# A diffusion backbone with an expert mixer: who makes the low parts of the weight tiles

## The chip, the cores and the metric

The kernel runs on one core of one Trainium2 chip. The metric is the device time of one execution in microseconds. The core has five engines with a queue of instructions each: TensorE (PE in the profile, its weight loads PEld), VectorE (DVE), ScalarE (ACT), GpSimd (POOL) and SyncE (SP). Each works through its own queue in order and waits at semaphores for the others.

## The reference

The model is a stack of two layers over a latent stream of 512 tokens and a context stream of 256 tokens, each token 1024 numbers in float32. A layer normalises and modulates, mixes tokens (a gated linear recurrence beside a short convolution, between an input and an output projection), and then runs an expert mixer, the PEER part:

```python
def peer_ffn(h, wq, subkeys, u, v):
    qr = (h @ wq).reshape(bsz, t, PEER_HEADS, 2, PEER_HALF)
    scores = jnp.einsum('bthpd,hpkd->bthpk', qr, subkeys)
    s1, i1 = lax.top_k(scores[..., 0, :], PEER_TOPK)
    s2, i2 = lax.top_k(scores[..., 1, :], PEER_TOPK)
    ...
    top, pos = lax.top_k(cand, PEER_TOPK)       # 16 of 16 x 16 sums
    eidx = jnp.take_along_axis(cidx, pos, axis=-1)
    gate = jax.nn.softmax(top, axis=-1)
    ...
        act = jax.nn.gelu(jnp.einsum('ted,td->te', u[ek], hk), approximate=False)
        return jnp.einsum('te,ted->td', gk * act, v[ek])
```

Each token chooses 8 x 16 = 128 of 16384 experts; an expert is one row of `u` and one row of `v`. The context stream is needed in layer 0 in full, and in layer 1 only for the final states of the recurrence.

## The kernel before

**Precision by splitting.** TensorE multiplies in a rounded format (`float32r`). So every operand is split into a high part (the rounded copy) and a low part (the rest), and each product is three matmuls: high by high, high by low, low by high. For a weight tile this is done by `weights` (L289 to L298): SP's queue loads 512 KB into `wraw` (L293), ScalarE rounds it into `whi` (L295), and a subtraction on one engine makes `wlo` (L297). Each of the three has three buffers. `weights` is called for 624 tiles of 128 x 1024: by `proj` for the projections of mixing and of the expert queries, by `experts_in` for the rows of `u`, by `dense` for the rows of `v`.

**Two ways through the experts.** For most token blocks of 128 (three or four of a layer) the mixer is computed densely, over all experts: `gates` makes a table of gate values by token and expert (one-hot tiles `oA`, `oB`, L759 to L776, multiplied on TensorE into `gps` and written to memory as `gd`); `experts_in` multiplies the tokens by two tiles of `u` and applies the GELU (`A`); `dense` multiplies `A` by the gates (L809), splits it into `Wh` and `Wl` (L812, L813), and for each group of 8 expert tiles and each of 8 output slices multiplies by a tile of `v` (L820 to L822) and adds the sum to the residual `resx` (L824). Some of the `experts_in` work is done ahead, during `gates`, and kept in memory (`ad`).

For the remaining blocks (two context blocks in layer 0, one latent block in layer 1) `gather_block` fetches the chosen rows: for each of 128 choices GpSimd issues an indirect transfer of one row of `u` for every token (L856, into three buffers `gr` and one `gs`), and VectorE multiplies it with the tokens and sums (L863); then the same for `v`, with an accumulating VectorE operation (L872). These 256 gathers for a block run beside `gates` and `dense` of the same layer. The result is added to the residual at L877 and L879.

**Who sets the order.** The program is written stage by stage, but a planner places the instructions in each engine's queue by a modelled timeline and priorities; weight tiles have a raised priority (`WPRIO`), and gathers fill in. What an engine is asked to do therefore changes the order planned for all of them. The order of the streams in the mixing of layer 1 puts the latent stream first.

**What the change touches.** Two constants, `POOL_LO` and `POOL_UT`, decide in `dense` and in `experts_in` which engine makes a tile's low part; without them it is VectorE.

Of the kernel before, what the change touches and what calls it, by code (L numbers as in the profile page):

```python
# [9 lines left out]
F = mybir.dt.float32  # L10
# [5 lines left out]
OP = mybir.AluOpType  # L16
# [25 lines left out]
U0 = 96  # L42
EARLY = (1, 0)
LASTK = [4, 5, 6, 7, 0, 1, 2, 3]
POOL_LO = True
POOL_UT = True


class Streams:
# [7 lines left out]
class Kern:  # L57
# [9 lines left out]
            kw["reuse_waits"] = "tile"  # L67
        return (stack or self.ctx).enter_context(self.tc.tile_pool(name=name, bufs=bufs, **kw))

    # ---------------------------------------------------------------- constants  # L70
    def setup(self):
        nc, a = self.nc, self.a
        self.tables()
# [99 lines left out]
        tag = self.banks[self.turn % len(self.banks)]  # L173
        return self.psum(shape, tag, 2 if tag == "ga" else 1, name)

    # ---------------------------------------------------------------- adaLN
    def mods(self, l, cols, pool, tag, bufs, ptags=("mo",)):
        nc = self.nc
        for ct in cols:
            ptag = ptags[ct % len(ptags)]  # L180
            pp = self.psum([P, 512], ptag, 2 if ptag == "ga" else 1, "pmod")
            pt, pm = pp[:, :256], pp[:, 256:].rearrange("p (a b) -> p a b", b=P)
            for kh in range(0, KC, 4):
                tags = tag.split()
                w = pool.tile([P, 4, 256], F, name="wmod", tag=tags[(2 * ct + kh // 4) % len(tags)], bufs=bufs)
                dma = nc.sync.dma_start(w, self.a["w_mod"][l, ct, :, kh:kh + 4])
                for k in range(4):
                    nc.tensor.matmul(pt[32 * k:32 * k + 32], self.cond[:, kh + k, :], w[:, k],
                                     start=kh == 0, stop=kh > 0, skip_group_check=True)
            part = self.wp.tile([P, 256], F, name="mpart", tag="mpart", bufs=1)  # L190
            nc.scalar.activation(part, pt, AF.Copy)
            for j in range(2):
                nc.tensor.matmul(pm[:, j], part[:, j * P:(j + 1) * P], self.selm, start=True, stop=True)
            c = ct * 2
            m = self.mod[l][:, c:c + 2, :]
            b = self.bmod[:, l, c:c + 2].unsqueeze(2).to_broadcast([P, 2, 2])
            nc.vector.tensor_tensor(m, pm[:, :, 0:2], b, op=OP.add)
            g, h = divmod(ct, 4)
            if g in (1, 4):
                n = 0 if g == 1 else 1  # L200
                s = self.scl[l][:, n, 2 * h:2 * h + 2]
                gb = self.ng[:, 2 * l + n, 2 * h:2 * h + 2].unsqueeze(2).to_broadcast([P, 2, 2])
                nc.vector.tensor_scalar(s, m, 1.0, None, op0=OP.add)
                nc.vector.tensor_tensor(s, s, gb, op=OP.mult)
        return dma.ins

    # ---------------------------------------------------------------- norms
    def rsqrt_rows(self, st, n, scale, name):
        nc = self.nc
        v = self.sm.tile([P, n], F, name=name + "v", tag="rv", bufs=2)  # L210
        s = self.sm.tile([P, n], F, name=name + "s", tag="rs", bufs=2)
        r = self.sm.tile([P, n], F, name=name + "r", tag="rr", bufs=2)
        nc.vector.tensor_scalar(v, st, scale, EPS, op0=OP.mult, op1=OP.add)
        nc.scalar.activation(s, v, AF.Ln)
        nc.scalar.activation(r, s, AF.Exp, scale=-0.5)
        nc.vector.scalar_tensor_tensor(s, v, 0.5, r, op0=OP.mult, op1=OP.mult)
        nc.vector.tensor_tensor(s, s, r, op=OP.mult)
        nc.vector.tensor_scalar(s, s, -1.0, 1.5, op0=OP.mult, op1=OP.add)
        nc.vector.tensor_tensor(r, r, s, op=OP.mult)
        return r  # L220
# [64 lines left out]
                eng = nc.gpsimd if POOL_NM and c % 2 else nc.vector  # L285
                eng.scalar_tensor_tensor(lo[:, c], t, sh[:, c:c + 1], hi[:, c].bitcast(F), op0=OP.add, op1=OP.subtract)

    # ---------------------------------------------------------------- projections
    def weights(self, src, eng=None):  # L289
        nc = self.nc  # L290
        with self.tc.high_priority(offset=WPRIO):
            raw = self.wp.tile([P, KC, P], F, name="wraw", tag="wraw", bufs=3)
            nc.sync.dma_start(raw, src)  # L293
            hi = self.wp.tile([P, KC, P], R, name="whi", tag="whi", bufs=3)
            nc.scalar.activation(hi, raw, AF.Copy)  # L295
            lo = self.wp.tile([P, KC, P], R, name="wlo", tag="wlo", bufs=3)
            (eng or nc.vector).tensor_tensor(lo, raw, hi.bitcast(F), op=OP.subtract)  # L297
        return hi, lo  # L298

    def mm3(self, out, w, a, n=None, order=range(KC)):  # L300
# [22 lines left out]
            out.append((pt[:, TX:TX + TC], slice(0, TC)))  # L323
        return out

    # ---------------------------------------------------------------- mixer
    def mixer(self, l):
        nc, a, tc = self.nc, self.a, self.tc
        last = l == self.depth - 1
# [252 lines left out]
        for src, sl in self.parts(pt, wc):  # L582
            nc.vector.tensor_tensor(self.oc.at(4 + j, sl.start, sl.stop), o[:, sl], src, op=OP.mult)

    # ---------------------------------------------------------------- PEER
    def top16(self, pool, vals, ixs, src, n):
        nc = self.nc
        w = pool.tile([P, n], F, name="mr", tag=f"mr{n}", bufs=1)
        nc.vector.max(vals[:, 0:8], src)
        nc.vector.max_index(ixs[:, 0:8], vals[:, 0:8], src)  # L590
        nc.vector.match_replace(w, vals[:, 0:8], src, NEG)
        nc.vector.max(vals[:, 8:16], w)
        nc.vector.max_index(ixs[:, 8:16], vals[:, 8:16], w)
# [187 lines left out]
    def experts_in(self, l, ap, hx, jp, nt):  # L781
        nc = self.nc
        pt = self.psum([P, 2, 512], "pj", 2, "p1")
        for t in range(2):
            w = self.weights(self.a["ut"][l, 2 * jp + t], self.nc.gpsimd if t and POOL_UT else None)
            self.mm3(pt[:, t, :nt], w, hx, nt)
        A = ap.tile([P, 2, nt], F, name="A", tag="A", bufs=3)
        self.gelus[0] = nc.scalar.activation(A, pt[:, :, :nt], AF.Gelu).ins  # L788
        return A

    def dense(self, l, es, ap, gd, ad, hx, nt):
        nc, a = self.nc, self.a
        dp = self.pool(f"pd{l}", stack=es)
        NG = 8
        for g in range(P // NG):
            ws = []
            for jp in range(NG // 2):
                j = g * NG + 2 * jp
                if j % 4 == 0:
                    gt = dp.tile([P, nt // 32, 4, 32], F, name="gt", tag="gt", bufs=2)  # L800
                    nc.sync.dma_start(gt.rearrange("p c i t -> p (c i t)"), gd[j // 4].rearrange("p c i t -> p (c i t)"))
                if j // 2 in AHEAD_SET[l]:
                    A = ap.tile([P, 2, nt], F, name="A", tag="A", bufs=3)
                    nc.sync.dma_start(A, ad[AHEAD_SET[l].index(j // 2)])
                else:
                    A = self.experts_in(l, ap, hx, j // 2, nt)
                for t in range(2):
                    av = A[:, t].rearrange("p (c t) -> p c t", t=32)
                    nc.vector.tensor_tensor(av, av, gt[:, :, j % 4 + t, :], op=OP.mult)  # L809
                wh = dp.tile([P, 2, nt], R, name="Wh", tag="Wh", bufs=NG // 2)  # L810
                wl = dp.tile([P, 2, nt], R, name="Wl", tag="Wl", bufs=NG // 2)
                nc.scalar.activation(wh, A, AF.Copy)  # L812
                nc.vector.tensor_tensor(wl, A, wh.bitcast(F), op=OP.subtract)  # L813
                ws.append((wh, wl))
            for c in range(KC):
                hi, lo = self.weights(a["vt"][l, c, g], nc.gpsimd if c % 2 and POOL_LO else None)
                pt = self.bank([P, nt], "p2")
                for j in range(NG):
                    wh, wl = (x[:, j % 2] for x in ws[j // 2])
                    nc.tensor.matmul(pt, hi[:, j], wh, start=j == 0, stop=False)  # L820
                    nc.tensor.matmul(pt, hi[:, j], wl, start=False, stop=False)  # L821
                    nc.tensor.matmul(pt, lo[:, j], wh, start=False, stop=j == NG - 1)  # L822
                dst = self.res.x[:, c, :nt]
                nc.vector.scalar_tensor_tensor(dst, pt, self.mod[l][:, 5 * KC + c, 0:1], dst, op0=OP.mult, op1=OP.add)  # L824
# [53 lines left out]
                dst = self.res.at(c, b * P, (b + 1) * P)  # L878
                nc.vector.scalar_tensor_tensor(dst, pt, self.mod[l][:, 5 * KC + c, s:s + 1], dst, op0=OP.mult, op1=OP.add)  # L879

    # ---------------------------------------------------------------- whole
    def final(self):
        nc = self.nc
        with ExitStack() as es:
# [91 lines left out]
```

## Time and profile before

| | |
|---|---|
| median of 3 runs | 4328.59 us |
| runs | 4332.73, 4328.59, 4319.31 us |
| span of the profiled execution | 4317.6 us, mean granted TensorE clock 0.969 |
| busy: TensorE, VectorE, ScalarE, GpSimd | 3993.6, 3522.3, 1747.0, 1854.1 us |
| low parts on VectorE | 368, 514.6 us |
| low parts on GpSimd | 256, 645.1 us |
| indirect transfers issued by GpSimd | 768 |
| moved to and from memory | 984.57 MB, mean 228 GB/s |

The profile gives the profiled execution from its first to its last instruction: its own time is that span, and what lies around it is seen only in the difference of 11.0 us to the median of the runs. An engine's busy time counts an instruction from its start to its end, also while it waits inside for something that it shares with another engine. The views that follow name instructions by line, engine and operation, with the tile written and the tiles read (`wlo<-wraw,whi`), the number of them after an x, and, in the views of groups, the total busy time, the mean in ns, and the idle time of the engine just before them with what ended it.

### The profile page before, as it was taken

The numbers are of one execution on the slowest core, as the hardware profiler recorded it, in microseconds if no ns is written. First come the engines' busy times: TensorE is split into PE (matmuls) and PEld (weight loads), VectorE is DVE, ScalarE is ACT, GpSimd is POOL, SyncE is SP. The second block draws the span as 40 slices with busy tenths as digits, with TensorE's granted clock in tenths as the row PEclk, the third lists the DMA queues.
The fourth block names the chain that finished last, engine by engine and source line by source line (L and its number), as shares of the span: only waits on it lengthen the run. The fifth ranks groups of instructions, "written<-read, shape, count | busy, mean of one in ns | idle before, by whom it ended". The sixth has DMA issues, their size and how long they took to land.

```text
span 4317.6 us, 59354 instructions
## 1 busy us (share of the span) xinstructions
PE 3993.6 (92%) x21357; PEld 3441.2 (80%) x21357; DVE 3522.3 (82%) x6416; ACT 1747.0 (40%) x2919; POOL 1854.1 (43%) x1180
## 2 busy tenths in 40 slices
PE   7999999989997999999989899979899989999997
PEld 5888778777885777777777778857899989999996
DVE  4766659999988999888788868758985788888987
ACT  4444332368772222222222245433598423333332
POOL 0211100244443566777667712110212257667675
PEclk9999999999998999999999999989999999999998
DMA  6444122489898898888888821213466679889896
GB/s 229 140 150 149 62 68 74 156 277 303 292 303 306 307 339 324 298 311 296 303 296 299 297 73 57 66 60 95 146 206 204 210 274 330 319 326 326 322 323 209
DMA packets 382167, 984.57 MB, mean 228 GB/s; under 512 B 30384, under 2 KB 161712, under 8 KB 377520
## 3 DMA queue, kind: packets, MB, share of 16 engines
q1 hardware_dynamic: 271280, 578.06, 39.1%
q0 software_dynamic: 110592, 402.70, 26.6%
q8 instruction: 169, 2.77, 0.3%
q14 instruction: 126, 1.03, 0.1%
HBM read 883.39 MB, written 97.26 MB: 227 GB/s over the span
## 4 chain that ended last, share of the span: by engine, by line
PE 46%; DVE 24%; DMA 11%; issue 9%; POOL 6%; ACT 3%; POOLq 0%; SPq 0%; DVEq 0%; ACTq 0%
PE p L822 5%; PE p L821 5%; PE p L820 5%; PE pj L304 5%; PE pj L305 5%; PE pj L306 5%; DMA gr<-in_v,picki 4%; DMA gr<-in_u,picki 4%; POOL wlo L297 3%; PE p L304 3%; PE p L305 3%; PE p L306 3%; DVE wlo L297 3%; POOL gr L856 2%; PE gps L775 2%
## 5 line engine op out<-in xcount | busy, mean ns | idle before, releaser
L295 ACT ACTIVATE whi<-wraw 128x1024 fp32r<-128x1024 f32 x624 | 654.5, 1057 | 1300.2 <-PE p L821 670.7
L297 POOL TENSOR_TENSOR wlo<-wraw,whi 128x1024 fp32r<-128x1024 f32 x256 | 645.1, 2521 | 913.1 <-ACT whi L295 329.9
L820 PE MATMUL p<-Wh,whi 128*128 128x512 f32 (+1 forms) x2048 | 753.4, 373 | 81.4 <-DVE resx L824 43.3
L822 PE MATMUL p<-Wh,wlo 128*128 128x512 f32 (+1 forms) x2048 | 755.1, 372 | 40.9 <-POOL wlo L297 24.9
L821 PE MATMUL p<-Wl,whi 128*128 128x512 f32 (+1 forms) x2048 | 759.7, 372 | 27.0 <-DVE Wl L813 26.9
L306 PE MATMUL p<-hxh,wlo 128*128 128x512 f32 (+1 forms) x2048 | 757.2, 370 | 15.0 <-POOL wlo L297 8.9
L304 PE MATMUL p<-hxh,whi 128*128 128x512 f32 (+1 forms) x2048 | 755.7, 369 | 0.7 <-ACT A L788 0.7
L305 PE MATMUL p<-hxl,whi 128*128 128x512 f32 (+1 forms) x2048 | 754.9, 369 | 0.0
L297 DVE TENSOR_TENSOR wlo<-wraw,whi 128x1024 fp32r<-128x1024 f32 x368 | 514.6, 1398 | 98.4 <-ACT whi L295 96.7
L856 POOL DMA_INDIRECT gr<-in_u,picki x312 | 412.3, 1322 | 414.3 <-DVE gr L863 321.6
L863 DVE SCALAR_TENSOR_TENSOR gr<-gr,htok 128x1024 f32<-128x1024 f32 x312 | 448.1, 1446 | 93.8 <-DMA gr<-in_u,picki 93.6
L872 DVE SCALAR_TENSOR_TENSOR acc<-gr,gw,acc 128x1024 f32<-128x1024 f32 x285 | 463.7, 1627 | 67.2 <-DMA gr<-in_v,picki 64.3
L856 POOL DMA_INDIRECT gr<-in_v,picki x288 | 400.2, 1390 | 269.4 <-DVE acc L872 190.3
L820 PEld LDWEIGHTS p<-Wh,whi 128*128 128x128 f32 x2048 | 393.1, 193 | 143.7 <-ACT Wh L812 46.3
L822 PEld LDWEIGHTS p<-Wh,wlo 128*128 128x128 f32 x2048 | 395.0, 193 | 100.0 <-POOL wlo L297 35.6
L821 PEld LDWEIGHTS p<-Wl,whi 128*128 128x128 f32 x2048 | 395.3, 193 | 80.0 <-DVE Wl L813 38.5
L306 PEld LDWEIGHTS p<-hxh,wlo 128*128 128x128 f32 x2048 | 388.3, 190 | 60.2 <-POOL wlo L297 13.2
L304 PEld LDWEIGHTS p<-hxh,whi 128*128 128x128 f32 x2048 | 388.6, 190 | 39.4 <-ACT A L788 1.0
L305 PEld LDWEIGHTS p<-hxl,whi 128*128 128x128 f32 x2048 | 388.5, 190 | 38.8
L812 ACT ACTIVATE Wh<-A 128x1024 fp32r<-128x1024 f32 (+1 forms) x128 | 122.0, 955 | 466.8 <-DVE A L809 429.6
L775 PE MATMUL gps<-oA,oB 128*128 128x128 f32 x1792 | 255.9, 279 | 32.3 <-DVE oA L767 23.9
L775 PEld LDWEIGHTS gps<-oA,oB 128*128 128x128 f32 x1792 | 245.1, 192 | 49.7 <-issue 11.5
(316 smaller groups left out, 7024.1 us busy)
## 6 DMA issues: line engine op xcount, KB each, us to landing
wraw<-in_ut SPq DMA_DIRECT2D x256, 512.0 KB
wraw<-in_vt SPq DMA_DIRECT2D x256, 512.0 KB
gd<-stg SPq DMA_DIRECT2D x28, 2048.0 KB
wmod<-in_w_mod SPq DMA_DIRECT2D x96, 512.0 KB
wraw<-in_w_in SPq DMA_DIRECT2D x64, 512.0 KB
gt<-gd SPq DMA_DIRECT2D x32, 1024.0 KB
gt<-gd SPq DMA_DIRECT2D x32, 768.0 KB
ad<-A SPq DMA_DIRECT2D x34, 512.0 KB
```

The source lines that it names most:

```text
L295: nc.scalar.activation(hi, raw, AF.Copy)
L297: (eng or nc.vector).tensor_tensor(lo, raw, hi.bitcast(F), op=OP.subtract)
L304: nc.tensor.matmul(out, wh[:, k], ah[:, k, :n], start=i == 0, stop=False)
L305: nc.tensor.matmul(out, wh[:, k], al[:, k, :n], start=False, stop=False)
L306: nc.tensor.matmul(out, wl[:, k], ah[:, k, :n], start=False, stop=i == KC - 1)
L775: nc.tensor.matmul(pt[:, s], B[:, s4 + s], A[:, s4 + s], start=True, stop=True)
L820: nc.tensor.matmul(pt, hi[:, j], wh, start=j == 0, stop=False)
L821: nc.tensor.matmul(pt, hi[:, j], wl, start=False, stop=False)
L822: nc.tensor.matmul(pt, lo[:, j], wh, start=False, stop=j == NG - 1)
L856: nc.gpsimd.indirect_dma_start(out=t, out_offset=None, in_=src, in_offset=bass.IndirectOffsetOnAxis(ap=eidx[:, e:e + 1], axis=0))
L863: nc.vector.scalar_tensor_tensor(u, u, 1.0, htok, op0=OP.mult, op1=OP.mult, accum_out=act[:, e:e + 1])
L872: nc.vector.scalar_tensor_tensor(acc, v, w[:, e:e + 1], acc, op0=OP.mult, op1=OP.add)
```

## The change

Every low part of a weight tile is made by VectorE. The two constants go, `weights` loses its choice of engine, and GpSimd keeps in these stages only the issues of the indirect transfers (and the small operations of the recurrence that it had). Comments that were changed beside it are left out.

```diff
-POOL_LO = True
-POOL_UT = True
...
-    def weights(self, src, eng=None):
+    def weights(self, src):
...
-            (eng or nc.vector).tensor_tensor(lo, raw, hi.bitcast(F), op=OP.subtract)
+            nc.vector.tensor_tensor(lo, raw, hi.bitcast(F), op=OP.subtract)
...
-            w = self.weights(self.a["ut"][l, 2 * jp + t], self.nc.gpsimd if t and POOL_UT else None)
+            w = self.weights(self.a["ut"][l, 2 * jp + t])
...
-                hi, lo = self.weights(a["vt"][l, c, g], nc.gpsimd if c % 2 and POOL_LO else None)
+                hi, lo = self.weights(a["vt"][l, c, g])
```

Before, the second of each pair of `u` tiles and every odd output slice of `v` went to GpSimd: 128 + 128 of the 624 tiles.

## The prediction

> **What bounds the kernel now.** First the page: span, busy shares, and the chain of work that ended last.
>
> ```profile
> span 4317.6 us, 59354 instructions
> PE 3993.6 (92%) x21357; PEld 3441.2 (80%) x21357; DVE 3522.3 (82%) x6416; ACT 1747.0 (40%) x2919; POOL 1854.1 (43%) x1180
> PE 46%; DVE 24%; DMA 11%; issue 9%; POOL 6%; ACT 3%; POOLq 0%; SPq 0%; DVEq 0%; ACTq 0%
> ```
>
> TensorE leads, VectorE is close behind, and GpSimd, although less than half busy, holds 6% of the chain. Second, the busy time by stretch. I cut the span at the stages: 850 to 1320 makes the gate tables of layer 0, 1320 to 2480 is its dense expert stage, 3100 to 3440 makes the gate tables of layer 1, 3440 to the end is its dense stage. The second fence is the same view for the weight tile `wlo` alone.
>
> ```profile
> core 0: us, PE busy (x) PEld busy (x) DVE busy (x) ACT busy (x) POOL busy (x), PEclk, DMA share, GB/s
> 850.00:1320.00 470.00, 423.12 (x2302) 360.63 (x2300) 432.73 (x787) 332.01 (x745) 212.04 (x145) 0.97 0.89 299
> 1320.00:2480.00 1160.00, 1062.22 (x4455) 851.58 (x4456) 1023.13 (x1181) 293.23 (x287) 767.48 (x482) 0.96 0.86 305
> 3100.00:3440.00 340.00, 329.03 (x2120) 325.57 (x2121) 241.61 (x584) 255.10 (x557) 74.17 (x29) 0.99 0.66 207
> 3440.00:4318.00 878.00, 811.13 (x4451) 778.65 (x4449) 758.48 (x838) 270.57 (x289) 584.22 (x347) 0.97 0.84 301
> ```
>
> ```profile
> 850.00:1320.00 470.00, 170.41 (x422) 80.96 (x422) 33.12 (x28) 65.88 (x27) 0.97 0.89 299
> 1320.00:2480.00 1160.00, 589.21 (x1482) 285.99 (x1482) 131.66 (x93) 231.28 (x93) 0.96 0.86 305
> 3100.00:3440.00 340.00, 159.17 (x459) 87.43 (x459) 35.32 (x29) 74.17 (x29) 0.99 0.66 207
> 3440.00:4318.00 878.00, 494.88 (x1471) 279.28 (x1470) 156.31 (x91) 229.97 (x91) 0.97 0.84 301
> ```
>
> In the first two stretches VectorE is busy for 92% and 88%. In 3100 to 3440 TensorE is (97%), and VectorE has 98 us to spare. GpSimd makes 27, 93, 29 and 91 low parts there: 240 of its 256.
>
> Third, the order of time around 2060 us (rows of the two engines, sorted by start).
>
> ```profile
> 2058.86 2.37 POOL L297 TENSOR_TENSOR wlo<-wraw,whi 128x1024 fp32r<-128x1024 f32 x1
> 2058.87 3.45 DVE L297 TENSOR_TENSOR wlo<-wraw,whi 128x1024 fp32r<-128x1024 f32 x1
> 2063.39 1.22 DVE L863 SCALAR_TENSOR_TENSOR gs<-gs,htok 128x1024 f32<-128x1024 f32 x1
> 2063.73 1.69 POOL L856 DMA_INDIRECT gr<-in_u,picki  x1 [2.51 <-DVE gr L863]
> 2070.04 0.94 POOL L856 DMA_INDIRECT gr<-in_u,picki  x1 [0.31 <-issue]
> ```
>
> A low part of VectorE that starts with one of GpSimd takes 3.45 us, the 2.37 us of the other and then its own 1.1. An indirect issue does no such harm: the operation beside it kept 1.22 us, and it was the issue that took 1.69 instead of 0.94. So what costs VectorE time is GpSimd's subtraction. How much it costs is the mean over the undisturbed median.
>
> ```profile
> L297 DVE TENSOR_TENSOR wlo<-wraw,whi x368: 1169/1217/4662, 42.7 to 4270.5; 128x1024 fp32r<-128x1024 f32 x184
> L297 POOL TENSOR_TENSOR wlo<-wraw,whi x256: 2346/2410/4405, 753.8 to 4272.7; 128x1024 fp32r<-128x1024 f32 x128
> L872 DVE SCALAR_TENSOR_TENSOR acc<-gr,gw,acc x285: 1266/1284/5418, 1399.8 to 4283.9; 128x1024 f32<-128x1024 f32 x143
> L863 DVE SCALAR_TENSOR_TENSOR gr<-gr,htok x312: 1164/1217/4101, 843.5 to 3883.5; 128x1024 f32<-128x1024 f32 x156
> L767 DVE TENSOR_SCALAR oA<-iota,gt,gt x448: 329/339/3158, 868.6 to 3356.1; 128x128 f32<-128x128 f32 x150
> ```
>
> **The change part by part.** Removed: 256 subtractions on GpSimd at a median of 2.410 us. Added: 256 on VectorE at 1.217 us, 311.6 us. No transfer, buffer or matmul changes; SP's 16 loads per dense group still wait for the same three `wraw` buffers, which a lo part of either engine releases. Behind an added lo part on VectorE's queue wait the gather operations, the evictions L824 and `Wl`; those wait for it at most 1.217 us. Behind the removed one on GpSimd's queue waited the indirect issues.
>
> *Gate tables of layer 0 (850 to 1320).* Groups of VectorE in this stretch, mean in ns after the busy time:
>
> ```profile
> L863 DVE SCALAR_TENSOR_TENSOR gr<-gr,htok 128x1024 f32<-128x1024 f32 x115 | 152.2, 1332 | 29.7 <-DMA gr<-in_u,picki 29.6
> L767 DVE TENSOR_SCALAR oA<-iota,gt,gt 128x128 f32<-128x128 f32 x256 | 99.4, 458 | 0.0
> L759 DVE TENSOR_TENSOR oB<-gt,iota 128x512 f32<-128x512 f32 x64 | 50.0, 787 | 0.8 <-PE gps L775 0.8
> L770 DVE TENSOR_TENSOR oA<-gt,iota 128x512 f32<-128x512 f32 x64 | 49.1, 766 | 0.0
> L646 DVE TENSOR_TENSOR oh<-oh,txf 128x512 f32<-128x512 f32 x30 | 20.4, 681 | 0.1
> ```
>
> The stretching is 115 x (1.332 - 1.217) = 13.2, 256 x (0.458 - 0.339) = 30.5, and against the 0.681 of an undisturbed 128x512 operation 64 x 0.106 = 6.8 and 64 x 0.085 = 5.4: 55.9 us given back. Added: 27 x 1.217 = 32.9. Net -23.0. VectorE is busy for 432.7 of the 470 us, and 29.6 of the other 37.3 go into waits for gathers (end of the first row), so I put all of it on the path.
>
> *Dense stage of layer 0 (1320 to 2480).*
>
> ```profile
> L872 DVE SCALAR_TENSOR_TENSOR acc<-gr,gw,acc 128x1024 f32<-128x1024 f32 x187 | 308.2, 1648 | 47.6 <-DMA gr<-in_v,picki 45.5
> L863 DVE SCALAR_TENSOR_TENSOR gr<-gr,htok 128x1024 f32<-128x1024 f32 x99 | 144.8, 1473 | 45.9 <-DMA gr<-in_u,picki 45.9
> L297 DVE TENSOR_TENSOR wlo<-wraw,whi 128x1024 fp32r<-128x1024 f32 x93 | 132.0, 1419 | 0.9 <-ACT whi L295 0.9
> L872 DVE SCALAR_TENSOR_TENSOR acc<-gs,gw,acc 128x1024 f32<-128x1024 f32 x63 | 100.5, 1595 | 13.8 <-DMA gs<-in_v,picki 13.1
> L813 DVE TENSOR_TENSOR Wl<-A,Wh 128x1024 fp32r<-128x1024 f32 x64 | 92.5, 1451 | 4.6 <-ACT Wh L812 4.4
> ```
>
> 187 x 0.364 + 99 x 0.256 + 93 x 0.202 + 63 x 0.311 + 64 x 0.234 = 68.1 + 25.3 + 18.8 + 19.6 + 15.0 = 146.8 given back; 93 x 1.217 = 113.2 added. Net -33.6, on the path: what VectorE does not work here it waits for gathers (104.5 in these rows).
>
> *Dense stage of layer 1 (3440 to the end).*
>
> ```profile
> L297 DVE TENSOR_TENSOR wlo<-wraw,whi 128x1024 fp32r<-128x1024 f32 x91 | 156.3, 1718 | 10.9 <-ACT whi L295 9.9 <-issue 1.0
> L872 DVE SCALAR_TENSOR_TENSOR acc<-gr,gw,acc 128x1024 f32<-128x1024 f32 x95 | 150.1, 1580 | 19.2 <-DMA gr<-in_v,picki 18.3
> L863 DVE SCALAR_TENSOR_TENSOR gr<-gr,htok 128x1024 f32<-128x1024 f32 x96 | 147.1, 1543 | 15.2 <-DMA gr<-in_u,picki 15.1
> L863 DVE SCALAR_TENSOR_TENSOR gs<-gs,htok 128x1024 f32<-128x1024 f32 x32 | 53.3, 1667 | 2.4 <-DMA gs<-in_u,picki 2.4
> L872 DVE SCALAR_TENSOR_TENSOR acc<-gs,gw,acc 128x1024 f32<-128x1024 f32 x32 | 49.9, 1561 | 2.6 <-DMA gs<-in_v,picki 2.1
> ```
>
> 91 x 0.501 + 95 x 0.296 + 96 x 0.326 + 32 x 0.450 + 32 x 0.277 = 45.6 + 28.1 + 31.3 + 14.4 + 8.9 = 128.3 given back; 91 x 1.217 = 110.7 added. Net -17.6.
>
> *The other 45 low parts* I cost at nothing: 29 lie in 3100 to 3440, where TensorE's 97% covers 29 x 1.217 = 35.3 us of VectorE (it has 98 to spare), and 16 in mixing and routing stretches. If that cover failed, +35.
>
> *Waits for gathers.* VectorE waits 29.6 + 104.5 + 37.9 = 172 us for them in the three stretches. GpSimd issues in order, and 211 low parts stand there among the issues of three blocks of 2 x 128 gathers, about one to four. The bounds are 0 (each issue waits for its buffer anyway) and a quarter of 172, -43. I take the middle, -20.
>
> *Gathers left over.* The order of VectorE's queue is written out by the planner, which will now count 256 more operations there and may set the gathers later. Now the last gather ends with the last dense matmul:
>
> ```profile
> L822 PE MATMUL p<-Wh,wlo x2048: 333/389/797, 1333.5 to 4283.5; 128*128 128x512 f32 x94, 128*128 128x384 f32 x93
> L872 DVE SCALAR_TENSOR_TENSOR acc<-gs,gw,acc x96: 1268/1284/4096, 1411.1 to 4285.2; 128x1024 f32<-128x1024 f32 x96
> ```
>
> Any gather set later in layer 1 is bare at 1.284 us. Bounds: 0, and 110.7 us if everything added in the stretch pushes gathers out. The row shows one trailing now, so I take a value near the lower end: 8 gathers, +10. The same push in layer 0 costs nothing, since the next layer's mixing begins with the latent stream and needs the gathered context later; without that cover it would cost up to 113.2.
>
> *TensorE's own waits for low parts* come on top of nothing. Of the views of waits one row names GpSimd's part in them:
>
> ```profile
> PEld p L822 <- POOL wlo L297: 35.6, 28, 2.0
> ```
>
> These 35.6 us fall into the same stretches whose length VectorE already sets, so counting them again would be counting twice. A low part will be ready 1.2 us after its high part instead of 2.4, but now always behind whatever gather VectorE is waiting for; what is late next for TensorE is then VectorE's own low part.
>
> Sum: -23.0 - 33.6 - 17.6 - 20 + 10 = -84. The profiled execution spans 4317.6 us; 11.0 us lie between that and the median of the runs, 4328.6. 4317.6 - 84 + 11 = 4245.
>
> **A rule weighed.** The row: an issue beside a two-input VectorE operation took 1.69 us, 0.75 more than alone. The Trainium skill ("SBUF — State Buffer", Who interferes with whom) infers that such an operation leaves descriptor generation alone, since it takes only the read side of the shared port; by that the moved operations delay no issue. This trace disagrees. By the row 211 x 0.75 = 158 us at most go onto GpSimd, which is idle for 944 us in the three stretches and is freed of 211 x 2.410 = 509 more; the sum stays.
>
> **The rivals.**
> *Leftover gathers (slower).* Place: after the last dense matmul of layer 1. All 110.7 us pushed out give 4235 + 111 = 4346 (4235 is the forecast without its own 10 us). It turns the gain to nothing at 73 gathers (94 us). For it: gathers and matmuls end together now. Against: VectorE really has less to do, and the gathers come off a queue with four buffers.
> *Starved issues (no change).* The 1.69 row on the path: if half of the 158 us is waited for by VectorE, 4245 + 79 = 4324. For it: VectorE's 172 us of waits, and DMA at 84 to 89% of its time. Against: GpSimd's idle time.
> *More than that (faster).* The waits for gathers halve, 86 instead of 20: 4179, with TensorE's 92% next in the way.
> That the edit does nothing is out: no call keeps another engine.
>
> **How the numbers follow.** Forecast 0.55 (4211 to 4291: from the three nets with -43 for the waits and no leftovers, -117, to half of the nets, -37), larger gain 0.12, starved issues 0.13, leftover gathers 0.20. The measurement tells about 0.3%, 13 us, from no change. Faster 0.67, same 0.13, slower 0.20. The range, 4165 to 4345, takes in the first three and leaves out most of the fourth.
>
> **What would show it.** Right: `wlo` on VectorE x624 near 1.22 us mean, L872 near 1.29, L767 near 0.34; VectorE's busy sum lower than 3522 by the nets, 74 us, or a little more, since the smaller groups are not in my sum; GpSimd at about 1200, its 1854 less the 645 us of the subtractions. Wrong: L872 after the last L822 for tens of us; longer waits of VectorE for `gr`; TensorE waiting for `wlo` for more than before; or operations still above their medians with GpSimd only issuing.

## The result, and the profile after

The changed kernel takes 4176.32 us, the median of 4 runs (4168.95 to 4183.52), against 4326.41 for the kernel before (4 runs, 4319.31 to 4332.73). The ratio is 0.965, 95% interval 0.9631 to 0.967: 150 us less, where 82 were forecast. The time lies in the stated range, near its lower end, and below the 4211 to 4291 that went with the forecast itself. First the head of the page of the changed kernel. Its lines are numbered two lower from `weights` on: L295 is `wlo`, L854 the indirect issue, L861 and L870 the two gather operations, L765 `oA`, L820 the last product of `dense`.

```profile
span 4181.8 us, 59060 instructions
PE 3942.6 (94%) x21357; PEld 3419.5 (82%) x21357; DVE 3392.2 (81%) x6672; ACT 1747.0 (42%) x2919; POOL 1203.1 (29%) x924
PE 50%; DVE 18%; issue 13%; DMA 10%; POOL 6%; ACT 2%; SPq 0%; POOLq 0%; DVEq 0%; ACTq 0%
```

VectorE took over 256 operations and its busy time fell by 130 us, from 3522.3 to 3392.2. GpSimd lost 651, and the chain moved from VectorE (24% to 18%) to TensorE (46% to 50%). Next the groups of VectorE over the whole span, kept apart by shape; after the bar stand the total busy time in us and the mean of one in ns. First before:

```profile
L297 DVE TENSOR_TENSOR wlo<-wraw,whi 128x1024 fp32r<-128x1024 f32 x368 | 514.6, 1398 | 98.4 <-ACT whi L295 96.7 <-issue 1.0
L872 DVE SCALAR_TENSOR_TENSOR acc<-gr,gw,acc 128x1024 f32<-128x1024 f32 x285 | 463.7, 1627 | 67.2 <-DMA gr<-in_v,picki 64.3
L863 DVE SCALAR_TENSOR_TENSOR gr<-gr,htok 128x1024 f32<-128x1024 f32 x312 | 448.1, 1446 | 93.8 <-DMA gr<-in_u,picki 93.6
L767 DVE TENSOR_SCALAR oA<-iota,gt,gt 128x128 f32<-128x128 f32 x448 | 162.7, 430 | 0.0
```

and after:

```profile
L295 DVE TENSOR_TENSOR wlo<-wraw,whi 128x1024 fp32r<-128x1024 f32 x624 | 762.0, 1225 | 109.2 <-ACT whi L293 107.5 <-issue 0.6
L861 DVE SCALAR_TENSOR_TENSOR gr<-gr,htok 128x1024 f32<-128x1024 f32 x312 | 378.5, 1221 | 80.2 <-DMA gr<-in_u,picki 79.2
L870 DVE SCALAR_TENSOR_TENSOR acc<-gr,gw,acc 128x1024 f32<-128x1024 f32 x285 | 365.4, 1282 | 54.5 <-DMA gr<-in_v,picki 52.7
L765 DVE TENSOR_SCALAR oA<-iota,gt,gt 128x128 f32<-128x128 f32 x448 | 124.3, 350 | 0.1
L870 DVE SCALAR_TENSOR_TENSOR acc<-gs,gw,acc 128x1024 f32<-128x1024 f32 x96 | 123.2, 1283 | 14.9 <-DMA gs<-in_v,picki 14.2
L861 DVE SCALAR_TENSOR_TENSOR gs<-gs,htok 128x1024 f32<-128x1024 f32 x72 | 87.8, 1220 | 28.0 <-DMA gs<-in_u,picki 27.7
```

The mean of every group shown now stands within 4% of the median that it had before: `wlo` 1.225 us (1.217), the gather operations 1.221 and 1.282 (1.217 and 1.284), `oA` 0.350 (0.339). So the stretching of these groups is gone; the longest gather operation on `gr` takes 1.326 us, where it took 5.418. The price can be read off: without `wlo` VectorE's busy time was 3522.3 - 514.6 = 3007.7 and is 3392.2 - 762.0 = 2630.2, so 377.5 came back; `wlo` itself gave back 514.6 - 368 x 1.217 = 66.7. Together 444 us, or 1.73 us of VectorE for each of GpSimd's 256 subtractions, while VectorE's own takes 1.22.

For the stages I cut both spans at the same events: the first gather operation, the start and end of each dense stage, and the first gate product of layer 1. Columns: the stretch and its length, then the busy time of each engine with its instructions, the granted clock, the share of the DMA engines, GB/s. First before:

```profile
843.00:1333.00 490.00, 430.14 (x2328) 365.90 (x2327) 450.58 (x839) 334.25 (x748) 219.46 (x150) 0.96 0.89 301
1333.00:2495.00 1162.00, 1075.78 (x4520) 862.78 (x4519) 1021.33 (x1142) 294.38 (x289) 768.40 (x480) 0.96 0.86 303
2495.00:3092.00 597.00, 541.80 (x2787) 448.48 (x2787) 458.40 (x1184) 261.17 (x448) 98.89 (x83) 0.95 0.23 75
3092.00:3397.00 305.00, 299.14 (x1977) 297.30 (x1977) 207.90 (x432) 249.56 (x559) 67.85 (x26) 0.99 0.67 209
3397.00:4286.00 889.00, 832.56 (x4610) 809.22 (x4608) 790.01 (x983) 275.48 (x290) 594.26 (x352) 0.98 0.85 303
4286.00:4318.00 32.00, 16.17 (x40) 5.23 (x40) 10.14 (x23) 8.61 (x13) 0.00 (x0) 0.68 0.18 66
```

and after:

```profile
851.00:1318.00 467.00, 423.93 (x2303) 362.26 (x2301) 409.59 (x813) 333.99 (x747) 152.15 (x121) 0.96 0.93 311
1318.00:2418.00 1100.00, 1052.79 (x4521) 852.43 (x4521) 967.95 (x1286) 294.11 (x288) 548.21 (x388) 0.98 0.90 320
2418.00:3019.00 601.00, 553.66 (x2858) 461.78 (x2855) 464.00 (x1204) 266.70 (x456) 75.72 (x76) 0.95 0.24 79
3019.00:3302.00 283.00, 283.00 (x1905) 282.81 (x1905) 202.09 (x442) 245.02 (x553) 0.00 (x0) 1.00 0.70 220
3302.00:4124.00 822.00, 809.34 (x4610) 798.05 (x4608) 732.80 (x1071) 273.83 (x289) 326.59 (x245) 1.00 0.88 319
4124.00:4182.00 58.00, 15.85 (x40) 5.27 (x40) 28.04 (x37) 8.62 (x13) 13.32 (x11) 0.61 0.45 152
```

| stage | before, us | after, us | length changes by | VectorE busy changes by |
|---|---|---|---|---|
| up to the first gather | 843 | 851 | +8 | +4 |
| gate tables, layer 0 | 490 | 467 | -23 | -41 |
| dense, layer 0 | 1162 | 1100 | -62 | -53 |
| mixing and routing, layer 1 | 597 | 601 | +4 | +6 |
| gate tables, layer 1 | 305 | 283 | -22 | -6 |
| dense, layer 1 | 889 | 822 | -67 | -57 |
| behind the last product | 32 | 58 | +26 | +18 |
| sum | 4318 | 4182 | -136 | -130 |

The profiled execution before was the fastest of its four runs (4319.31), the one after the slowest (4183.52), so the table shows 136 of the 150 us. A second profile of the changed kernel (span 4171.3) gives 850, 465, 1095, 598, 283, 824 and 56 us for the same seven stretches: changes of some 5 us in a row say nothing.

The two dense stages gave most. In that of layer 1 TensorE is now busy for 98%. The last stretch grew: there TensorE waits for gathers.

```profile
PE accT L875 <- DVE acc L870: 28.4, 1, 28.4
```

### The profile page after: what moved, and what is told of

It is laid out like the page before. It is cut to its first block, busy times and chain, and to the rows that moved or that the text cites. A ratio compares the mean times of both kernels' runs of the same rounds, so it can differ in the third digit from the quotient of the medians.

```text
span 4181.8 us, 59060 instructions
## 1 busy us (share of the span) xinstructions
PE 3942.6 (94%) x21357; PEld 3419.5 (82%) x21357; DVE 3392.2 (81%) x6672; ACT 1747.0 (42%) x2919; POOL 1203.1 (29%) x924
## 4 chain that ended last, share of the span: by engine, by line
PE 50%; DVE 18%; issue 13%; DMA 10%; POOL 6%; ACT 2%; SPq 0%; POOLq 0%; DVEq 0%; ACTq 0%
PE pj L302 5%; PE p L820 5%; POOL gr L854 5%; PE pj L303 5%; PE pj L304 5%; PE p L818 5%; PE p L819 5%; PE p L302 4%; PE p L303 4%; PE p L304 4%; DMA gr<-in_v,picki 4%; DVE wlo L295 3%; PE gps L773 2%; DMA gr<-in_u,picki 2%; DVE acc L870 2%
## 5 line engine op out<-in xcount | busy, mean ns | idle before, releaser
L854 POOL DMA_INDIRECT gr<-in_u,picki x312 | 410.7, 1316 | 1545.7 <-DVE picki L828 634.9
L295 DVE TENSOR_TENSOR wlo<-wraw,whi 128x1024 fp32r<-128x1024 f32 x624 | 762.0, 1225 | 109.2 <-ACT whi L293 107.5
L818 PE MATMUL p<-Wh,whi 128*128 128x512 f32 (+1 forms) x2048 | 738.6, 366 | 38.5 <-ACT Wh L810 20.1
L820 PE MATMUL p<-Wh,wlo 128*128 128x512 f32 (+1 forms) x2048 | 747.5, 367 | 18.3 <-DVE wlo L295 18.1
L819 PE MATMUL p<-Wl,whi 128*128 128x512 f32 (+1 forms) x2048 | 749.1, 366 | 16.0 <-DVE Wl L811 15.9
L854 POOL DMA_INDIRECT gr<-in_v,picki x288 | 393.1, 1365 | 426.1 <-DVE acc L870 313.3
L820 PEld LDWEIGHTS p<-Wh,wlo 128*128 128x128 f32 x2048 | 388.1, 190 | 72.9 <-DVE wlo L295 32.4
L861 DVE SCALAR_TENSOR_TENSOR gr<-gr,htok 128x1024 f32<-128x1024 f32 x312 | 378.5, 1221 | 80.2 <-DMA gr<-in_u,picki 79.2
L870 DVE SCALAR_TENSOR_TENSOR acc<-gr,gw,acc 128x1024 f32<-128x1024 f32 x285 | 365.4, 1282 | 54.5 <-DMA gr<-in_v,picki 52.7
L302 PE MATMUL pj<-h512h,whi 128*128 128x512 f32 x640 | 262.0, 412 | 12.3 <-ACT whi L293 4.6
```

The costliest lines, as they stand in the source:

```text
L295: nc.vector.tensor_tensor(lo, raw, hi.bitcast(F), op=OP.subtract)
L302: nc.tensor.matmul(out, wh[:, k], ah[:, k, :n], start=i == 0, stop=False)
L854: nc.gpsimd.indirect_dma_start(out=t, out_offset=None, in_=src, in_offset=bass.IndirectOffsetOnAxis(ap=eidx[:, e:e + 1], axis=0))
L861: nc.vector.scalar_tensor_tensor(u, u, 1.0, htok, op0=OP.mult, op1=OP.mult, accum_out=act[:, e:e + 1])
L870: nc.vector.scalar_tensor_tensor(acc, v, w[:, e:e + 1], acc, op0=OP.mult, op1=OP.add)
```

## The experiments

**Theory A:** a GpSimd subtraction costs by what it does to the VectorE operation beside it. **Rival B:** GpSimd's low parts come late, and TensorE waits for them. **Rival C:** GpSimd's being busy, or holding buffers and delaying issues and loads, is what costs.

**One half at a time.** Each takes one of the two constants of the kernel before.

```diff
-POOL_UT = True
+POOL_UT = False      # e1_u_only
```
```diff
-POOL_LO = True
+POOL_LO = False      # e2_v_only
```

> Only the low parts of the u tiles go to VectorE (128 of the 256); those of v stay on GpSimd. Theory A (each GpSimd subtraction lengthens the VectorE operation beside it, wherever it stands): the gain is shared by place. By the stage lengths of the two traces, the dense stages gained 62 + 67 us less 26 of bare tail and hold 64 v tiles to about 28 u tiles each; the gate stages, with u tiles alone, gained 33. So u alone is worth 0.32 x 103 + 33 = 66 us: about 4260. Rival B (TensorE waited for the late low parts of GpSimd themselves): in the waits of before, those at the v products were two thirds or more, so u alone is worth about 45 us: about 4281. Theory A also says that L767 keeps near 0.34 us in the gate stages, while L872 and L863 in the dense stages stay stretched.

> Only the low parts of the v tiles go to VectorE; those of u stay on GpSimd as before. Theory A: 0.68 x 103 = 70 us, about 4256, and the sum of the two halves equals the whole, 150. Rival B: about 105 us, near 4221. Theory A also says that L767 stays stretched (mean near 0.43 us) and that the stretching of L872 and L863 in the dense stages falls to about a third.

Measured: u alone 4261.24 us (ratio 0.9848, 0.9831 to 0.9864), v alone 4258.17 (0.9849, 0.9832 to 0.9866), the kernel before 4326.75 beside them. That is 66 and 69 us, within some 2 us of theory A; rival B's 45 and 105 are out. How near the figures come is partly by construction, since theory A's shares were worked out from the stage lengths of the result; the test is how the gain divides. The halves were also to sum to 150. They sum to 134, and what the other 15 or so consist of was not tried. The place of the gain can be read from the traces, cut at the same events; these are the changes of length against the kernel before, in us:

| stage | u alone | v alone | both |
|---|---|---|---|
| gate tables, layer 0 | -22 | -1 | -23 |
| dense, layer 0 | -11 | -43 | -62 |
| gate tables, layer 1 | -21 | -1 | -22 |
| dense, layer 1 | -28 | -24 | -67 |
| behind the last product | +8 | -1 | +26 |

The gate stages follow the u tiles alone, as theory A says. Groups of VectorE, u tiles alone moved:

```profile
L872 DVE SCALAR_TENSOR_TENSOR acc<-gr,gw,acc 128x1024 f32<-128x1024 f32 x285 | 428.1, 1502 | 52.6 <-DMA gr<-in_v,picki 49.9
L767 DVE TENSOR_SCALAR oA<-iota,gt,gt 128x128 f32<-128x128 f32 x448 | 126.5, 351 | 0.1
```

v tiles alone moved:

```profile
L872 DVE SCALAR_TENSOR_TENSOR acc<-gr,gw,acc 128x1024 f32<-128x1024 f32 x285 | 387.1, 1358 | 50.3 <-DMA gr<-in_v,picki 47.6
L767 DVE TENSOR_SCALAR oA<-iota,gt,gt 128x128 f32<-128x128 f32 x448 | 162.4, 428 | 0.0
```

`oA` is made only in the gate stages, where GpSimd has u tiles alone: with those gone it is undisturbed (0.351), with the v tiles gone it is stretched as before (0.428 against 0.430). The gather operation of the dense stages keeps two thirds of its stretching in the first kernel (1.502 from 1.627, undisturbed 1.284) and a fifth in the second (1.358), where a third was forecast.

**The stretching without the waiting.** GpSimd works again, but no product uses what it makes. The second kernel has GpSimd as busy, in the same place, with writes alone.

```diff
             nc.vector.tensor_tensor(lo, raw, hi.bitcast(F), op=OP.subtract)
+            if also:      # t == 1 for u, c % 2 == 1 for v; e3_raw_read
+                nc.gpsimd.tensor_tensor(raw, raw, hi.bitcast(F), op=OP.subtract)
```
```diff
             nc.vector.tensor_tensor(lo, raw, hi.bitcast(F), op=OP.subtract)
+            if also:      # e5_raw_memset
+                for part in (raw, raw, raw[:, :KC // 2]):
+                    nc.gpsimd.memset(part, 0.0)
```

> The changed kernel, and after the VectorE subtraction of the same 256 tiles GpSimd subtracts once more, in place into wraw, a result that nobody reads. No matmul waits for GpSimd here; only the load into that wraw buffer and the indirect issues behind it do. Theory A: the 418 us of stretching that the trace of before shows come back, or more, since each such operation now starts just behind a VectorE operation and meets the next: 1.6 to 2.4 us each, 4176 + 400 to 600 less what VectorE's idle time swallows: 4450 to 4750, with L872 back to 1.6 us or over. Rival B (late low parts, and the planner's order): nothing waits for it, 4176 to 4210. Rival C (longer held wraw buffers, delayed issues): as slow as the run with memsets in the same place.

> The changed kernel, and after the VectorE subtraction of the same 256 tiles GpSimd overwrites wraw with zeros in two memsets of 128x1024 and one of 128x512, some 2.4 us in all, by the 0.74 us of a 128x768 memset in the trace. GpSimd is as busy as with the second subtraction and holds wraw as long, but reads nothing from SBUF. Theory A with reading as the cause: VectorE's two-input operations keep 1.22 and 1.28 us, and the time stays within 4176 to 4230 (later loads, later issues). If any GpSimd work that holds SBUF is the cause: as slow as the second subtraction. L765 (one input) may be the exception either way.

Measured: with the subtraction 4508.03 us (2 runs, 4508.0 and 4508.06), some 181 above the kernel before and 332 above the changed one; with the memsets 4214.65 (4206.35 to 4221.21), 38 above the changed one. Groups of the kernel with the second subtraction (each kernel's own line numbers):

```profile
L297 POOL TENSOR_TENSOR wraw<-wraw,whi 128x1024 f32<-128x1024 f32 x256 | 699.5, 2732 | 1059.1 <-DVE wlo L295 914.7 <-issue 106.2 <-DMA wraw<-in_ut 17.1
L863 DVE SCALAR_TENSOR_TENSOR gr<-gr,htok 128x1024 f32<-128x1024 f32 x312 | 477.8, 1541 | 82.2 <-DMA gr<-in_u,picki 81.9
L872 DVE SCALAR_TENSOR_TENSOR acc<-gr,gw,acc 128x1024 f32<-128x1024 f32 x285 | 455.7, 1599 | 53.6 <-DMA gr<-in_v,picki 51.4
L767 DVE TENSOR_SCALAR oA<-iota,gt,gt 128x128 f32<-128x128 f32 x448 | 158.9, 421 | 0.0
```

and with the memsets:

```profile
L298 POOL MEMSET wraw<- 128x1024 f32 x512 | 492.0, 961 | 999.0 <-DVE wlo L295 979.3 <-DMA wraw<-in_ut 4.9
L298 POOL MEMSET wraw<- 128x512 f32 x256 | 139.0, 543 | 5.2
L864 DVE SCALAR_TENSOR_TENSOR gr<-gr,htok 128x1024 f32<-128x1024 f32 x312 | 377.1, 1218 | 89.7 <-DMA gr<-in_u,picki 89.0
L873 DVE SCALAR_TENSOR_TENSOR acc<-gr,gw,acc 128x1024 f32<-128x1024 f32 x285 | 365.0, 1281 | 74.0 <-DMA gr<-in_v,picki 72.4
L768 DVE TENSOR_SCALAR oA<-iota,gt,gt 128x128 f32<-128x128 f32 x448 | 145.9, 458 | 0.1
```

The gather operations are stretched to 1.541 and 1.599 us beside reading (1.446 and 1.627 before the change) and untouched beside 631 us of memsets (1.218 and 1.281). So the reading alone is enough: the whole loss came back, and more, with no product waiting for GpSimd's result. Rival B is not needed for it. A share of the 150 us it can still have: before the change TensorE stood waiting for GpSimd's low parts for 24.9 us in `dense` (a row below) and 8.9 in `experts_in`, 33.8 in all, and no run separates these. Rival C, tested as a whole, is worth 38 us here. Part of what it consists of shows in the waits of ScalarE for its loads, in the kernel with memsets and then in the changed one:

```profile
ACT whi L293 <- DMA wraw<-in_vt: 288.7, 89, 14.0
```
```profile
ACT whi L293 <- DMA wraw<-in_vt: 85.0, 18, 8.7
```

A `wraw` buffer held 2.4 us longer makes the next load later. The other 293 us between the two kernels go with the reading: VectorE is busy for 3835.5 us beside the subtractions and for 3413.9 beside the memsets. The two are not alike in all else, since `wraw` is held for 2.73 us by the subtraction and for 2 x 0.961 + 0.543 = 2.47 by the memsets. The forecast of theory A held: it had 400 to 600 us of stretching, less what VectorE's idle time swallows, 4450 to 4750. VectorE's busy time rose by 3835.5 - 3392.2 = 443 against the changed kernel, near the lower end, and the time by 332. That the subtraction starts right behind a VectorE operation did not make it worse than before: 443 / 256 = 1.73 us each.

**The bare tail.** In the changed kernel the last product of the dense stage starts at 4122.3 us and the last gather operation at 4149.7. These are rows of the views of the two lines: minimum, median and maximum in ns, first and last start in us.

```profile
L820 PE MATMUL p<-Wh,wlo x2048: 334/389/797, 1318.7 to 4122.3; 128*128 128x512 f32 x94, 128*128 128x384 f32 x93
L870 DVE SCALAR_TENSOR_TENSOR acc<-gs,gw,acc x96: 1267/1280/1331, 1395.7 to 4149.7; 128x1024 f32<-128x1024 f32 x96
```

Three kernels move pairs of u tiles between the gate stage and the dense stage.

```diff
-AHEAD = (34, 30)
+AHEAD = (34, 26)     # e4_ahead26; (34, 24) in e4_ahead24
```
```diff
-AHEAD = (34, 30)
-SPAN = (34, 60)
+AHEAD = (38, 26)     # e6_ahead38
+SPAN = (38, 60)
```

> The changed kernel beside the next three on one chip: 4168 to 4184, as before; its last matmul of the dense stage is followed by some 28 us in which TensorE waits for the last gathers.

> The changed kernel with 26 instead of 30 pairs of u tiles of layer 1 multiplied ahead, in the gate stage; four pairs move into the dense stage. A pair is 48 matmuls of 0.172 us from start to start in the trace (128x384): 33 us of TensorE move from a stage where it is 100% busy to one where it is 98% busy and the gathers end 28 us too late. Theory A (the tail is bare because the dense stage got shorter than the gathers): the gate stage loses 33 us, the dense stage gains 33, the tail goes from 28 to near 0: 4176 - 28 = about 4150. Rival (the planner spreads the gathers over whatever length the dense stage has): the tail stays, about 4176.

> The same with 24 pairs: 50 us move, more than the tail has. Theory A: no better than with 26, 4145 to 4160, with no tail left. Rival: about 4176.

> 26 pairs ahead in layer 1 and 38 instead of 34 in layer 0. Four pairs of 48 matmuls at 0.226 us, 43 us, move from the dense stage of layer 0 (TensorE busy 96%) into its gate stage, where TensorE has 43 us to spare but VectorE is busy for 88% and the transfers for 93%. If TensorE's slack there can be used: up to 40 us below the run with 26, about 4115. If VectorE or the transfers bound that stage: its added loads and low parts (8 x 1.2 us) lengthen it, and the gathers of layer 0, which end with the dense stage now, come to stand bare behind it: 4150 to 4180.

Measured on one chip: the changed kernel 4179.69 us (5 runs, 4168.08 to 4182.02; its tail again 27.5 us), 26 pairs 4169.77 (5 runs, 4164.7 to 4176.13), 24 pairs 4174.87, 38 and 26 pairs 4178.67. The ratios to the kernel before are 0.9653 (0.9637 to 0.9669), 0.9637 (0.9623 to 0.9651), 0.9651 and 0.965. With 26 pairs, from the same two views:

```profile
L820 PE MATMUL p<-Wh,wlo x2048: 333/389/796, 1311.2 to 4138.9; 128*128 128x512 f32 x94, 128*128 128x384 f32 x93
L870 DVE SCALAR_TENSOR_TENSOR acc<-gs,gw,acc x96: 1265/1279/1322, 1387.4 to 4106.7; 128x1024 f32<-128x1024 f32 x96
```

The tail is gone, the gathers now end 32 us ahead of the products, and yet the time is only 10 us lower, with overlapping intervals: better or equal is not settled. Theory A of the tail was right on the cause and wrong on the worth: it had 4150 for 26 pairs and 4145 to 4160 for 24. The gate stage with its lead-in became 24 us shorter (283 to 259), not 33, and the dense stage 47 us longer (822 to 869), more than the 33 us of products moved:

```profile
3012.00:3271.00 259.00, 251.06 (x1716) 250.38 (x1715) 186.10 (x382) 234.26 (x541) 0.00 (x0) 0.99 0.71 220
3271.00:4140.00 869.00, 849.11 (x4808) 834.06 (x4806) 768.93 (x1152) 285.79 (x302) 354.97 (x256) 1.00 0.86 311
4140.00:4164.00 24.00, 9.24 (x32) 3.85 (x31) 6.74 (x14) 7.13 (x11) 0.00 (x0) 0.70 0.23 87
```

TensorE is busy for 97 and 98% of these two stretches: what one stage loses the other pays. In layer 0, where four more pairs went into the gate stage, nothing was gained either: 4178.67, which is 9 us above the run with 26 pairs, with overlapping intervals.

## Why the prediction was right, and where its sizes were off

*The mechanism* held: GpSimd's subtraction stretches VectorE's operation, an indirect issue does not, and doing the work on VectorE costs less than the stretching did. The signs named for it came: `wlo` at 1.225 us, L872's operation at 1.282, L767's at 0.350, GpSimd at 1203. But 150 us came where 82 were forecast, outside the forecast's own 4211 to 4291. The number lies beside the rival "More than that", 4179, and that is chance: its way was that the waits for gathers fall by 86 us, and they fell by 17.

*The nets.* The terms -23.0, -33.6 and -17.6 (74 us of VectorE) were too small: its busy time fell by 41, 53 and 57, of which 18 only moved into the tail. I had summed the five dearest groups of a stretch and left the rest out; over the whole span the given back is 444 us and not the 331 of my rows.

*On the path.* For the gate tables of layer 0 the length came out as forecast (-23), although VectorE saved 41 there: by luck, a net that was too small met a path that passed on only part of it. For the dense stages I had put the nets on the path, as if VectorE alone set their length, and counted TensorE's own waits as nothing on top. There the length fell by more than VectorE's busy time: 62 and 67. That is the term that failed most. TensorE was the busier of the two there already, for 93 and 94% against VectorE's 88 and 89%. Its time without work fell from 86 us (1162 - 1076) to 47 (1100 - 1053) in layer 0 and from 56 (889 - 833) to 13 (822 - 809) in layer 1, where the stage ended bounded by TensorE. Two of the waits that shrank, before and after:

```profile
PE p L822 <- POOL wlo L297: 24.9, 25, 1.5
PE p L820 <- DVE resx L824: 43.3, 24, 4.8
```
```profile
PE p L820 <- DVE wlo L295: 18.1, 32, 2.2
PE p L818 <- DVE resx L822: 18.2, 14, 3.8
```

The waits for GpSimd's low parts went, and those for VectorE's hardly grew (15.8 before). The rest of the shortening, 23 us in each dense stage, is TensorE's busy time itself, with the same matmuls: 1076 to 1053 and 833 to 809. The granted clock, the share of its full speed that TensorE was allowed, rose there from 0.96 to 0.98 and from 0.98 to 1.00. By these rounded figures an estimate is 1162 x 0.04 - 1100 x 0.02 = 24 us and 889 x 0.02 = 18, so most of it. The prediction had no term for this, and why the clock rose was not tried.

*At nothing.* The gate tables of layer 1 were to be covered by TensorE. They became 22 us shorter, with the mixing before them 4 us longer. The rows show why: 72 matmuls fewer stand in the gate stage (1977 to 1905) and 71 more in the stage before (2787 to 2858), so the planner set them earlier, and TensorE's 6 us of idle time vanished. With the v tiles alone moved, that stage stays as it was (304 us, 1977 matmuls), and with the u tiles alone it is 284 us with 1912; so this belongs to the u tiles and, by the matmuls, to the order, and I had not foreseen it. Why the planner moved them was not tried.

*Waits for gathers.* Forecast -20. In the groups after, the waits for `gr` and `gs` sum to 79.2 + 52.7 + 14.2 + 27.7 = 173.8, before over the whole span to 93.6 + 64.3 + 15.2 + 17.8 = 190.9: -17. That is near, but -20 was only the middle between two bounds. The rival of starved issues did not come: the waits did not grow.

*Leftover gathers.* Forecast +10 by 8 gathers. It came as the rival described it, at a smaller size: 15 gather operations start behind the last product, where two did before, and that stretch grew by 26. It stayed well short of the 94 us that would have undone the gain, and what its removal brought, 10 us, is within the spread of the runs.

*Around the span.* The changed kernel's profiled run took 4183.52 us over a span of 4181.8: 1.7 us lie around it. So of the 11.0 us that I put there for the kernel before, some 9 were the difference between that execution and the median. Against spans the change is worth 136 us, against medians 150.

## What to carry to other kernels

Work given to a free engine is free only if it does not slow the busy one: compare the mean of the busy engine's operations with their undisturbed median, and put the difference on the bill of the offloaded work. Here 2.41 us on an engine that was 43% busy cost VectorE 1.73 us, and doing the work there costs 1.22. Then ask which engine sets the length of the stage: here TensorE's waits shrank together with VectorE's work, and the gain was larger than VectorE's net. When the bound engine is relieved, look next at whatever the planner had fitted to its old length: gathers that ended with a stage now stand behind it.

## What the runs showed of the hardware

GpSimd's writing alone is not harmless for every VectorE operation. Beside memsets the two-input operations kept 1.218, 1.281 and, in the group of `wlo`, 1.22 us, but `oA`, a one-input `tensor_scalar` between two SBUF tiles, went from 0.350 to 0.458 us, further than beside the subtractions before the change (0.430). The Trainium skill ("SBUF — State Buffer", Who interferes with whom) makes this distinction: two SBUF inputs contend with a GpSimd instruction that reads SBUF and not with one that only writes, while the faster two-port mode of `tensor_scalar` contends with GpSimd without that condition. These runs agree with both halves, as far as they show them: in which mode `oA` ran stands in no row, but a `tensor_scalar` of 128x1024 (L868, the first of each `acc`) took 0.748 us where the two-input L870 took 1.280.

The page also infers that `tensor_tensor`, taking only the read side of the shared ports, leaves descriptor generation alone. For these indirect issues that does not hold: the row of 1.69 us before the change stood beside the two-input L863, and after the change the same happens beside `tensor_tensor` itself. Around 2015 us of the changed kernel, in order of time (start and duration in us), GpSimd and then VectorE:

```profile
2011.12 0.94 POOL L854 DMA_INDIRECT gr<-in_u,picki  x1 [0.60 <-DVE gr L861]
2018.81 0.94 POOL L854 DMA_INDIRECT gr<-in_u,picki  x1 [3.79 <-DVE gr L861]
2020.62 1.69 POOL L854 DMA_INDIRECT gr<-in_u,picki  x1 [0.86 <-DVE gr L861]
```
```profile
2018.46 0.75 DVE L822 SCALAR_TENSOR_TENSOR resx<-p,mod,resx 128x512 f32<-128x512 f32 x1
2020.26 1.22 DVE L295 TENSOR_TENSOR wlo<-wraw,whi 128x1024 fp32r<-128x1024 f32 x1
2021.40 1.22 DVE L861 SCALAR_TENSOR_TENSOR gr<-gr,htok 128x1024 f32<-128x1024 f32 x1
```

An issue that finds VectorE idle (2011.12) or at the eviction L822, which takes one of its inputs from PSUM (2018.81), needs 0.94 us. One that finds it at a low part (2020.62) ends at 2022.31: 0.91 behind 2021.40, when the low part gives way to the next operation, and not held up again by the gather operation that starts then. An issue also reads its row numbers (`picki`) from a tile; whether that reading waits or the making of the descriptors, no run here separates. The reverse delay does not show: beside 768 issues the 597 gather operations on `gr` took 1.326 us at most. So with the subtractions gone nothing on GpSimd stretched them any more, and the issues on `gr` stayed near their means (1.316 and 1.365 us, from 1.322 and 1.390).
